# Two uneven stores in place of one: giving four DMA engines more rows at step 56 and at the last step

## The chip, the cores and the metric

The kernel runs on one core of one Trainium2 chip. The time is that of the device in microseconds (us), first as the median of a kernel's runs. "Span" is the time from the first to the last instruction of the profiled execution; it is about 1.8 us shorter than that execution's time.

## The reference

Inputs `q` and `k` are float32 of (16, 512, 16, 64): batch, sequence, heads, dimension. Both are rotated, then each position's heads are multiplied with all positions of the same head:

```python
q_rot = concatenate([q1 * cos - q2 * sin, q1 * sin + q2 * cos], axis=-1)   # k alike
scores = einsum('bshd,bthd->bsht', q_rot, k_rot)                          # (16, 512, 16, 512) float32
```

The output is 268 MB, the inputs 67 MB.

## The kernel before

There are 64 steps (`NST`), 16 batches of 4 (`C`). A step makes 128 rows of 16 heads of 512 scores, 4 MB, in one of three stage buffers in turn, so step i may write its scores only when the store of step i - 3 has landed. For each pair of heads TensorE (PE) multiplies, and ScalarE (ACT) copies the scores from PSUM to the stage.

```python
        for i in range(C, NST):
            ...
            st = stage(i)                       # one of three buffers
            for p in range(HP):
                scores(slot("q", i)[:, P * p : P * (p + 1)], block("k", b, p), st[:, 2 * p : 2 * p + 2])
                ...                             # transposes and rotations for later steps
            store(i, st)
            ...                                 # two of four steps load q or k of a later batch
```

From step 4 on, every store but the last is one transfer of 128 rows (the first four steps, of the first batch, store in two parts). The last leaves two heads of its rows to transfers of their own:

```python
    def last(o, st):
        h = H - 2
        nc.sync.dma_start(o[:, :h], st[:, :h])           # 128 rows of 14 heads: all 16 DMA engines
        nc.sync.dma_start(o[:116, h:], st[:116, h:])     # 116 rows: 29 on each of four engines
        nc.sync.dma_start(o[116:, h:], st[116:, h:])     # 12 rows: one on each of twelve engines
    def store(i, st):
        b, c = divmod(i, C)
        if i == NST - 1:
            last(o_v[b, :, c], st)
        else:
            nc.sync.dma_start(o_v[b, :, c], st)
```

The comments say what the trace of this kernel shows at the last store: 8 long rows on every engine, thirty 4 KB rows (29 and one) on four engines, one on each of eight more, none on the last four.

Of the kernel before, what the change touches and what calls it, by code (L numbers as in the profile page):

```python
# [10 lines left out]
def kernel(  # L11
# [13 lines left out]
    B, S, H, D = q.shape  # L25
# [3 lines left out]
    HP = H // 2  # L29
    NST = B * C  # L30
    G = H // C
    R = H - G

    const_pool = ctx.enter_context(tc.tile_pool(name="const", bufs=1))
# [11 lines left out]
    o_v = out.rearrange("b (p c) h t -> b p c h t", c=C)  # L46
# [4 lines left out]
    ss_t = const_pool.tile([P, C, 2, HD], fp32, name="ss_t")  # L51
    ss_v = ss_t.rearrange("p c x j -> p c (x j)")

    def last(o, st):

        h = H - 2
        nc.sync.dma_start(o[:, :h], st[:, :h])
        nc.sync.dma_start(o[:116, h:], st[:116, h:])
        nc.sync.dma_start(o[116:, h:], st[116:, h:])



    RW = R * S
    W = H * S
# [5 lines left out]
    def stage(i):  # L70
        at = (3 * RW, 0, W)[(i - C) % 3]
        return stage_t[:, at : at + W].rearrange("p (h t) -> p h t", t=S)

    def store(i, st):
        b, c = divmod(i, C)
        if i == NST - 1:
            last(o_v[b, :, c], st)
        else:
            nc.sync.dma_start(o_v[b, :, c], st)

# [22 lines left out]
    def slot(which, n):  # L103
        if which == "r":
            return first["q"][:, n, G * D :]
        t, c = tiles[which, n]
        return t[:, c]

    def unit(which, n):
        return which != "r" and n < C  # L110

    def rope(which, n):
# [4 lines left out]
        if unit(which, n):  # L117
            x = first[which][:, :, G * D * n : G * D * (n + 1)]
            cs = cos_t.unsqueeze(2).to_broadcast((P, C, 2 * G, HD))
            ss = ss_v.unsqueeze(2).to_broadcast((P, C, G, D))  # L120
            sv, k1, k2 = "p c (g j) -> p c g j", {"j": HD}, {"j": D}
# [51 lines left out]
    def scores(lhs, rhs, so):  # L173


        ps = ps_s_pool.tile([P, 2, S], fp32, tag="ps_s", name="ps")
        for r in range(2):
            nc.tensor.matmul(  # L178
                out=ps[:, r, :].rearrange("s (c t) -> s c t", c=C),
                lhsT=lhs[64 * r : 64 * r + 64],  # L180
                rhs=rhs[64 * r : 64 * r + 64],
                start=True,
                stop=True,
            )
        nc.scalar.copy(  # L185
            out=so.rearrange("s r (t c) -> s r t c", c=C),
            in_=ps.rearrange("s r (c t) -> s r t c", c=C),
        )
# [9 lines left out]
    with tc.manual_schedule():  # L198
# [13 lines left out]
        for p in range(HP):  # L212
            c, hp = divmod(p, 2)
            scores(block("q", 0, hp)[:, c], block("k", 0, hp), st_all[:, 2 * p : 2 * p + 2])
            if hp == 1:
                nc.sync.dma_start(o_v[0, :, c, :G], st_all[:, G * c : G * (c + 1)])
            if p == 3:
# [9 lines left out]
        for i in range(C):  # L227
            st = st_rest[i]
# [3 lines left out]
            else:  # L232
                dve = rope("q", C) + rope("k", C + i) + rope("q", C + 1) + rope("k", 2 * C)
                nxt = [("q", C), ("k", C + i)]
            for p in range(R // 2):
                scores(
# [14 lines left out]
        for i in range(C, NST):  # L251
            b, c = divmod(i, C)
            tr = {}
            if i + 1 < NST:
                tr[1], tr[3] = ("q", i + 1, 0), ("q", i + 1, 1)
            if i + C < NST:
                tr[5], tr[6] = ("k", i + C, 0), ("k", i + C, 1)
            dve = []
            if i + 2 < NST:
                dve += rope("q", i + 2)  # L260
            if i + 1 + C < NST:
                dve += rope("k", i + 1 + C)
            st = stage(i)
            for p in range(HP):
                scores(slot("q", i)[:, P * p : P * (p + 1)], block("k", b, p), st[:, 2 * p : 2 * p + 2])
                if p not in tr:
                    continue
                if tr[p][0] == "q":
                    run(dve[:1])
                    dve = dve[1:]  # L270
                    transposed(*tr[p], nc.vector.tensor_copy)
                else:
                    transposed(*tr[p], nc.scalar.copy)
            run(dve)
            store(i, st)
            if c == 1 and b > 1:
                load("q", b + 2)
            elif c == C - 1:
                load("k", b + 3)
# [30 lines left out]
```

## Time and profile before

| | before |
|---|---|
| time, first three runs | 801.64 us (800.84 to 802.97) |
| span of the profiled run | 800.1 us |
| busy: PE, DVE, ACT | 86%, 68%, 71% |
| moved by DMA | 336.19 MB at 420 GB/s |

How to read it: no compute engine is full, while the row of DMA shares in the slices is at nine tenths or more in all slices but the last. A sixteenth of that share is one DMA engine, and with a mean over sixteen engines the tail of a few of them is hard to see in a slice of 20 us. The lines are in the prediction below; the windows cut around the end are what show it. A packet counts whole in the window in which it starts, so in windows of a microsecond or two the share is rough: one engine at work shows as 0.04 to 0.06.

Two moments are used from here on. **R** is when step 54's store has landed on the slowest engine, which lets step 57's score copies begin; it is the end of the wait that starts at 680.72 in the chain (680.72 + 30.02 = 710.74). **X** is when the engines that wait for step 57's store start it, 722.38 here. The slowest engine is called **L**, and the four engines with thirty of the short rows are "the four". The times of single DMA packets come from the trace's packet records, strung into chains as the prediction tells.

### The profile page before, as it was taken

Reading aid. Unit: us, or ns where it says so; the run is one execution under the profiler, and the core shown is the slowest. Engines: PE = TensorE matmul, PEld = TensorE weight load, DVE = VectorE, ACT = ScalarE, POOL = GpSimd, SP = SyncE. Lnnn points to the kernel's source line nnn. Section 1 sums busy time; section 2 is a strip of 40 time slices with the busy share of each in tenths; the row PEclk is TensorE's granted clock in tenths of the full one; section 3 lists DMA queues with packets and bytes.
Section 4 is the critical chain, followed back from the end, with each engine's and each line's share of the span. In section 5 each row is a group of like instructions: output and inputs, shape, how many; then the busy total and the mean of one; then the engine's idle time right before and its main releaser. Section 6 shows DMA issues by size and latency. Waiting matters only on the chain.

```text
span 800.1 us, 8186 instructions
## 1 busy us (share of the span) xinstructions
PE 688.1 (86%) x3072; PEld 298.5 (37%) x3072; DVE 541.6 (68%) x510; ACT 564.1 (71%) x655; POOL 0.7 (0%) x6
## 2 busy tenths in 40 slices
PE   1999999978889978998889888898988979889960
PEld 1444443433334433443333333343433334334420
DVE  4999988856677756785666866667666677577300
ACT  1898887767677756777667676676866768668870
POOL 0000000000000000000000000000000000000000
PEclk9999999989998988998989989899898998899995
DMA  9999999999999999999999999999999999999996
GB/s 369 418 434 429 433 435 426 427 417 430 430 435 430 426 427 427 437 433 424 430 432 428 436 423 439 423 435 427 435 428 434 410 425 436 405 391 396 421 420 249
DMA packets 15158, 336.19 MB, mean 420 GB/s; under 512 B 1680, under 2 KB 1936, under 8 KB 2320
## 3 DMA queue, kind: packets, MB, share of 16 engines
q1 hardware_dynamic: 14832, 335.55, 98.3%
q8 instruction: 24, 0.39, 0.2%
q10 hardware_dynamic: 288, 0.13, 0.1%
q14 instruction: 14, 0.11, 0.0%
HBM read 67.24 MB, written 268.44 MB: 420 GB/s over the span
## 4 chain that ended last, share of the span: by engine, by line
DMA 46%; PE 45%; ACT 5%; issue 1%; DVE 0%; ACTq 0%; SPq 0%; DVEq 0%
DMA out_dram<-st 45%; PE ps L178 34%; PE bank L170 11%; ACT st L185 4%; DMA st<-in_k_dram 1%; ACT st L171 0%; ACTq L305 0%; DVE st L148 0%; DVE st L144 0%; DVE part L143 0%; SPq L99 0%; ACTq L185 0%; DVEq L143 0%
## 5 line engine op out<-in xcount | busy, mean ns | idle before, releaser
L185 ACT COPY st<-ps 128x1024 f32<-128x1024 f32 x512 | 495.1, 1019 | 197.3 <-DMA out_dram<-st 102.8
L178 PE MATMUL ps<-k_sb,q_sb 64*128 64x512 f32 x1920 | 513.7, 652 | 71.3 <-ACT st L185 71.3
L178 PEld LDWEIGHTS ps<-k_sb,q_sb 64*128 64x128 f32 x1920 | 172.4, 197 | 248.2 <-issue 137.9
L171 DVE COPY q_sb<-bank 128x512 f32<-128x512 f32 x118 | 81.5, 691 | 202.3 <-PE bank L170 202.3
L170 PEld LDWEIGHTS bank<-ident,q_sb 128*128 128x128 f32 x480 | 55.6, 152 | 102.3 <-issue 100.0
L170 PE MATMUL bank<-ident,q_sb 128*128 128x128 f32 x480 | 86.7, 308 | 0.0
L170 PEld LDWEIGHTS bank<-ident,k_sb 128*128 128x128 f32 x480 | 50.5, 141 | 91.2 <-DVE k_sb L144 39.6
L170 PE MATMUL bank<-ident,k_sb 128*128 128x128 f32 x480 | 78.0, 286 | 0.0
L144 DVE TENSOR_TENSOR k_sb<-k_sb,cos_t 128x1024 f32<-128x1024 f32 x60 | 73.5, 1225 | 2.9
L144 DVE TENSOR_TENSOR q_sb<-q_sb,cos_t 128x1024 f32<-128x1024 f32 x60 | 73.5, 1225 | 2.1
L148 DVE TENSOR_TENSOR k_sb<-k_sb,part 128x1024 f32<-128x1024 f32 x60 | 73.5, 1225 | 2.1
L143 DVE TENSOR_TENSOR part<-q_sb,ss_t 128x1024 f32<-128x1024 f32 x60 | 73.5, 1225 | 2.0
L143 DVE TENSOR_TENSOR part<-k_sb,ss_t 128x1024 f32<-128x1024 f32 x60 | 72.9, 1216 | 0.2
L148 DVE TENSOR_TENSOR q_sb<-q_sb,part 128x1024 f32<-128x1024 f32 x60 | 72.9, 1215 | 0.1
L171 ACT COPY k_sb<-bank 128x512 f32<-128x512 f32 x120 | 71.4, 600 | 0.0
L178 PE MATMUL ps<-st 64*128 64x512 f32 x128 | 32.7, 639 | 0.4 <-ACT st L171 0.4
L170 PE MATMUL bank<-ident,st 128*128 128x128 f32 x64 | 10.7, 317 | 16.7 <-DVE st L148 13.2
L171 ACT COPY st<-bank 128x512 f32<-128x512 f32 (+1 forms) x18 | 9.2, 566 | 13.7 <-PE bank L170 13.7
L143 DVE TENSOR_TENSOR part<-st,ss_t 128x1024 f32<-128x1024 f32 (+1 forms) x9 | 10.0, 1106 | 10.5 <-DMA st<-in_k_dram 9.2
L178 PEld LDWEIGHTS ps<-st 64*128 64x128 f32 x128 | 11.7, 197 | 13.7 <-issue 8.0
L170 PEld LDWEIGHTS bank<-ident,st 128*128 128x128 f32 x64 | 8.2, 161 | 21.9 <-issue 16.4
L148 DVE TENSOR_TENSOR st<-st,part 128x512 f32<-128x512 f32 (+1 forms) x14 | 10.3, 765 | 0.3
(11 smaller groups left out, 13.8 us busy)
## 6 DMA issues: line engine op xcount, KB each, us to landing
out_dram<-st SPq DMA_DIRECT2D x59, 4096.0 KB, 24.7
k_sb<-in_k_dram SPq DMA_DIRECT2D x15, 2048.0 KB, 28.3
q_sb<-in_q_dram SPq DMA_DIRECT2D x15, 2048.0 KB, 26.9
out_dram<-st SPq DMA_DIRECT2D x4, 3072.0 KB, 18.3
out_dram<-st SPq DMA_DIRECT2D x4, 1024.0 KB, 12.4
out_dram<-st SPq DMA_DIRECT2D x1, 3584.0 KB, 21.4
st<-in_q_dram SPq DMA_DIRECT2D x1, 2048.0 KB, 11.9
st<-in_k_dram SPq DMA_DIRECT2D x2, 512.0 KB, 5.4
```

Of the source, the lines that this page charges most:

```text
L143: nc.vector.tensor_tensor(pv, xs, ss, op=mult)
L144: nc.vector.tensor_tensor(xc, xc, cs, op=mult)
L148: nc.vector.tensor_tensor(y, y, z, op=add)
L170: nc.tensor.transpose(bank[:, y, :], x[:, y], ident)
L171: copy(out=x, in_=bank[:, :m])
L178: nc.tensor.matmul(out=ps[:, r, :].rearrange("s (c t) -> s c t", c=C), lhsT=lhs[64 * r : 64 * r + 64], rhs=rhs[64 * r : 64 * r + 64], star ...
L185: nc.scalar.copy(out=so.rearrange("s r (t c) -> s r t c", c=C), in_=ps.rearrange("s r (c t) -> s r t c", c=C),)
```

## The change

It means to take bytes off L in a second place: at step 56, whose store is followed by a time in which most DMA engines wait (the DMA share is 0.24 from 719.4 to 721.0 us and 0.06 from 721.0 to 722.3), and a little more in the last store. The whole of it:

```diff
+    UNEVEN = {NST - 8: 2, NST - 1: 3}
...
-    def last(o, st):
-
-        h = H - 2
+    def uneven(o, st, heads):
+
+        h = H - heads
         nc.sync.dma_start(o[:, :h], st[:, :h])
         nc.sync.dma_start(o[:116, h:], st[:116, h:])
         nc.sync.dma_start(o[116:, h:], st[116:, h:])
...
-        if i == NST - 1:
-            last(o_v[b, :, c], st)
+        if i in UNEVEN:
+            uneven(o_v[b, :, c], st, UNEVEN[i])
```

## The prediction

> **What bounds the kernel now.** I read the page first: the slices, the chain that ended last, the DMA queues.
>
> ```profile
> PE   1999999978889978998889888898988979889960
> ...
> DMA  9999999999999999999999999999999999999996
> GB/s 369 418 434 429 433 435 426 427 417 430 430 435 430 426 427 427 437 433 424 430 432 428 436 423 439 423 435 427 435 428 434 410 425 436 405 391 396 421 420 249
> ...
> q1 hardware_dynamic: 14832, 335.55, 98.3%
> q8 instruction: 24, 0.39, 0.2%
> ...
> DMA out_dram<-st 45%; PE ps L178 34%; PE bank L170 11%; ACT st L185 4%; DMA st<-in_k_dram 1%; ACT st L171 0%; ACTq L305 0%; DVE st L148 0%; DVE st L144 0%; DVE part L143 0%; SPq L99 0%; ACTq L185 0%; DVEq L143 0%
> ```
>
> The 16 DMA engines are busy in nearly every slice; the load is 336 MB and cannot shrink. What can be lost is only the time in which some of the 16 are idle. So I looked at the end, in windows, reading the DMA share times 16 as the number of engines still at work.
>
> ```profile
> 717.00:718.00 1.00, 1.00 (x8) 0.72 (x8) 0.96 (x2) 1.00 (x2) 0.00 (x0) 1.00 0.54 229
> 718.00:719.40 1.40, 1.40 (x10) 0.54 (x8) 1.37 (x2) 1.31 (x3) 0.00 (x0) 1.00 0.33 140
> ...
> 721.00:722.30 1.30, 1.30 (x8) 0.43 (x5) 0.34 (x1) 1.30 (x2) 0.00 (x0) 1.00 0.06 25
> ...
> 781.00:789.50 8.50, 0.00 (x0) 0.00 (x0) 0.00 (x0) 0.00 (x0) 0.00 (x0) 0.50 1.00 429
> ...
> 792.00:795.20 3.20, 0.00 (x0) 0.00 (x0) 0.00 (x0) 0.00 (x0) 0.00 (x0) 0.50 0.32 113
> ...
> 796.30:798.50 2.20, 0.00 (x0) 0.00 (x0) 0.00 (x0) 0.00 (x0) 0.00 (x0) 0.50 0.04 15
> 798.50:800.10 1.60, 0.00 (x0) 0.00 (x0) 0.00 (x0) 0.00 (x0) 0.00 (x0) 0.50 0.00 0
> ```
>
> From 781 to 789.5 us compute has ended and all sixteen engines stream. From 792 to 795.2 the share is 0.32: five engines. From 796.3 to 798.5 it is 0.04: one engine alone. The last 1.6 us are the landing and the program's end. So one straggler sets the end, and four others follow it closely.
>
> The trace's records of single DMA packets say who they are. A packet of a row starts 3 to 4 ns before the one ahead of it on its engine ends, so they can be strung into chains. The straggler, which I call L, ends the store of step 62 at 789.61 us, where the others end it at 781.4; then it moves eight 28 KB rows, one 4 KB row, and ends at 798.50. L has exactly one 4 KB row; four chains have thirty, and end at 795.28, 795.64, 796.20 and 796.25; the rest end at 790 to 792. L ends the stores of steps 57, 58, 59 and 60 at 740.15, 750.13, 760.13 and 770.06, with no idle time, at 10.0 us a store against 9.7 for the others (its packets of 32 KB took 1213 to 1251 ns, most others' 1213). It is behind because it is a little slower all along, and it has not waited since well before 600 us. Its bytes are the bound.
>
> The other engines wait for L, by way of the stage buffers:
>
> ```profile
> 680.72 30.02 DMA out_dram<-st
> ...
> 750.21 20.38 DMA out_dram<-st
> 770.58 0.02 issue
> 770.61 0.04 ACTq L185
> ```
>
> In the chain of waits the score copy of step 57 starts only when the store of step 54 has landed on L, at 710.7; that of step 63 when step 60's has, at 770.6. The late start of step 57 makes the hole at 717 to 722.4 us: the share falls to 0.06, only L at work, and fifteen engines start step 57's store within 143 ns at 722.4.
>
> [...] 4 KB rows took 159 ns when undisturbed and up to 727 at 790 us, and L's last eight 28 KB rows took 1062, 1069, 1062, 1062, 1180, 1076, 1062 and 1178 ns, 255 ns more than eight of 1062.
>
> **The change, part by part.** Nothing moves on PE, DVE or ACT; the queue of SP gets two more transfers at step 56. In KB for each engine:
>
> - Step 56 was 8 rows of 32 KB, 256 for all. Now 8 x 28 = 224, plus 29 x 4 = 116 and 4 on engines 0 to 3 (344), plus 4 on engines 4 to 11 (228); engines 12 to 15 have 224.
> - Step 63 already was 344, 228 and 224. Now 8 x 26 = 208, plus 29 x 6 + 6 = 180 on engines 0 to 3 (388), plus 6 (214), or 208.
> - Together +132 KB for engines 0 to 3, -28 - 14 = -42 for 4 to 11, where L is, and -48 for 12 to 15. The total is unchanged (4 x 132 = 8 x 42 + 4 x 48).
>
> L's gain: at step 56 eight rows go from 1213 to 1062 ns, 1.21 us less, and a 4 KB row of 0.16 is added: 1.05. At step 63 eight rows lose another 2 KB each; 4 KB are 151 ns (1213 less 1062), so 75 ns a row, 0.60 us, less 0.07 for the longer single row: 0.53. Sum 1.58. [...] L should end 1.2 us earlier, near 797.3. All of it is on the path, as L never waits.
>
> Engines 0 to 3 at step 63: eight rows of 26 KB at 987 ns are 7.9 us instead of 8.5, so they reach their extra rows at 789.35 instead of 789.95. The thirty rows took 5.3 to 6.3 us before, where thirty undisturbed ones at 155.5 ns would take 4.7: 1.14 to 1.35 times. Rows of 6 KB should start 231 ns apart (159 + 75.5 - 3.5), thirty of them 6.9 us, and 7.9 to 9.3 with that hindrance. They end at 797.2 to 798.7, if step 56 leaves them nothing to catch up.
>
> Step 56 gives them 88 KB more, 30 x 0.156 - 8 x 0.151 = 3.5 us. Nine engines ended step 56 at 717.9 us and then idled 4.5 until 722.4: for such an engine it is all hidden. The later stores leave almost no idle time (0.1 to 0.4 us before steps 58 and 59, none after), so nothing else can absorb it.
>
> So on my main path the end goes from 798.5 to the later of L, 797.3, and the slowest of the four, near 798: half a microsecond less. 801.6 becomes about 801.1.
>
> **Rivals.**
>
> 1. The four take over as the bound by more. Four engines of the sixteen ended step 56 not at 717.9 but at 721.1 to 721.3. If these are engines 0 to 3, only 1.1 us of idle time is left, of 3.5, and the rest collides with step 57's packets; some 2.4 to 3 us, less 0.6 of later holes, is carried to the end, which becomes about 800.4: 1.9 us slower, 803.5. For it: a group of just four that keep together. Against it: the trace does not number the engines, the hole cuts the chains at 722.4, and other groups of four fit as well. I give it a quarter.
> 2. [...] L gains nothing. For it: the 1180 and 1178 ns packets. Against it: 255 ns for eight rows, not 1200. It would make 801.6 to 802.
> 3. Everything goes well: the four's rows are hindered as little as the best chain was, and L's gain is whole. End 796.9 to 797.3, 800.2.
> 4. The extra issues delay the queue. Step 63's took 0.33, 0.71 and 1.21 us on SP, and SP waits for ACT 654 us in all; step 57 is issued 10 us later. Nothing.
>
> **Range and chances.** Weighing 1 at a quarter, 2 at a fifth and the main path and 3 for the rest gives 801.1 in the middle, with more room above. The three runs of before spread by 2.1 us, as much as the effect itself. The range that should hold 8 times in 10 is 799.6 to 802.9. A change of 2% would be 16 us, ten times the 1.58 us that L sheds, so within 2% is 0.99, and 0.005 for each side.
>
> **What would show it.** In the windows after the last issue, the time with one engine alone (0.04 to 0.06) should go or be short, and five engines (about 0.3) should be at work until some 797. At 717 to 722 us the share should rise to five engines or so instead of falling. L's last packet should end near 797.3 and the landing of step 60 come about 0.8 us earlier than 770.6. If the four end after 799 rival 1 holds; if L's end does not move, rival 2. The prediction is wrong altogether if L is another engine in the next execution, one of the first four, say, or if its lag comes from something that the bytes do not govern.

No trace numbers the engines. "Engines 0 to 3", "4 to 11" and "12 to 15" are names of the groups that the trace shows: four engines with thirty 4 KB rows, eight with one (L among them), four with none. That step 56's store would divide in the same way was a forecast; the changed kernel's trace shows four chains that move thirty 4 KB rows there and end at 721.5 to 721.7. L's gain came to 1.58 us, less 0.4, the estimate of further delay: the 255 ns by which L's last eight rows exceeded eight of 1062 ns, once more at step 56, and half as much at step 63. That leaves 1.2, and L's end near 797.3.

## The result, and the profile after

| | before | after |
|---|---|---|
| median of six runs each | 801.51 us (800.84 to 802.97) | 801.83 us (799.68 to 804.69) |
| ratio | | 1.0003, 95% interval 0.998 to 1.0026 |
| span of the profiled run | 800.1 us | 800.5 us |
| L's last byte, us of the span | 798.50 | 797.02 |
| last byte of the four | 796.25 | 798.65 |

The ratio is the mean time of one kernel's fast runs over that of the other's of the same rounds, so it is not quite the ratio of the two medians.

The changed kernel's windows, of the same kind as the prediction shows for the kernel before (stretch, its length, busy time of PE, PEld, DVE, ACT and POOL, granted clock, DMA share, GB/s):

```profile
717.30:719.40 2.10, 2.10 (x12) 0.88 (x10) 2.06 (x2) 1.69 (x2) 0.00 (x0) 0.83 0.56 232
...
720.50:721.70 1.20, 1.20 (x8) 0.61 (x8) 1.17 (x2) 1.20 (x2) 0.00 (x0) 1.00 0.28 113
721.70:723.80 2.10, 2.10 (x12) 0.82 (x9) 0.56 (x1) 1.96 (x3) 0.00 (x0) 1.00 0.06 27
...
792.00:796.80 4.80, 0.00 (x0) 0.00 (x0) 0.00 (x0) 0.00 (x0) 0.00 (x0) 0.50 0.31 123
797.05:798.20 1.15, 0.00 (x0) 0.00 (x0) 0.00 (x0) 0.00 (x0) 0.00 (x0) 0.50 0.25 102
798.70:800.50 1.80, 0.00 (x0) 0.00 (x0) 0.00 (x0) 0.00 (x0) 0.00 (x0) 0.50 0.01 5
```

Before, one engine was alone at the end (0.04 from 796.3 to 798.5). Now, after L is done at 797.02, the share is 0.25: four engines of sixteen. In the hole after step 56 the share is 0.28 up to 721.7, five engines: L and the four with their extra rows. Then L is alone, 0.06, until X at 723.91. So the four's extra work of step 56 was hidden in full, and their extra work of step 63 made them the last.

The chain of waits shows R, 681.81 + 29.26 = 711.07:

```profile
681.81 29.26 DMA out_dram<-st
711.17 1.02 ACT st L186
```

From R on, the two traces can be compared step by step on L, which has no idle time in either:

| L, us | before | after |
|---|---|---|
| step 56's store | 9.98 (720.15 to 730.13) | 8.92 (720.46 to 729.38) |
| steps 57 to 62 | 59.48 | 59.53 |
| step 63 | 8.89 | 8.11 |
| end, counted from R | 87.76 | 85.95 |

L sheds 1.06 + 0.78 us, and ends 1.8 us earlier counted from R. The four end 0.18 us before L's old place: 798.65 - 711.07 = 87.58. That is nearly all of the gain given back.

### The profile page after: what moved, and what is told of

Same layout as the page of the kernel before. It is cut to its first block, busy times and chain, and to the rows that moved or that the text cites. A ratio compares the mean times of both kernels' runs of the same rounds, so it can differ in the third digit from the quotient of the medians.

```text
span 800.5 us, 8190 instructions
## 1 busy us (share of the span) xinstructions
PE 690.9 (86%) x3072; PEld 300.2 (38%) x3072; DVE 541.6 (68%) x510; ACT 564.4 (71%) x655; POOL 0.7 (0%) x6
## 4 chain that ended last, share of the span: by engine, by line
PE 46%; DMA 45%; ACT 4%; DVE 2%; issue 1%; ACTq 0%; SPq 0%; DVEq 0%
DMA out_dram<-st 43%; PE ps L179 35%; PE bank L171 11%; ACT st L186 3%; DMA st<-in_q_dram 1%; DVE st L149 1%; DVE part L144 1%; DVE st L145 1%; ACTq L306 0%; SPq L100 0%; ACTq L186 0%; ACT st L172 0%; DVEq L144 0%
## 5 line engine op out<-in xcount | busy, mean ns | idle before, releaser
L145 DVE TENSOR_TENSOR k_sb<-k_sb,cos_t 128x1024 f32<-128x1024 f32 x60 | 73.5, 1225 | 2.9
L145 DVE TENSOR_TENSOR q_sb<-q_sb,cos_t 128x1024 f32<-128x1024 f32 x60 | 73.5, 1225 | 2.1
L149 DVE TENSOR_TENSOR k_sb<-k_sb,part 128x1024 f32<-128x1024 f32 x60 | 73.5, 1225 | 2.1
L144 DVE TENSOR_TENSOR part<-q_sb,ss_t 128x1024 f32<-128x1024 f32 x60 | 73.5, 1225 | 2.0
L144 DVE TENSOR_TENSOR part<-k_sb,ss_t 128x1024 f32<-128x1024 f32 x60 | 73.0, 1216 | 0.2
L179 PEld LDWEIGHTS ps<-st 64*128 64x128 f32 x128 | 11.4, 192 | 13.4 <-issue 7.6
```

The costliest lines, as they stand in the source:

```text
L144: nc.vector.tensor_tensor(pv, xs, ss, op=mult)
L145: nc.vector.tensor_tensor(xc, xc, cs, op=mult)
L149: nc.vector.tensor_tensor(y, y, z, op=add)
L179: nc.tensor.matmul(out=ps[:, r, :].rearrange("s (c t) -> s c t", c=C), lhsT=lhs[64 * r : 64 * r + 64], rhs=rhs[64 * r : 64 * r + 64], star ...
```

## The experiments

Twelve runs were made. Nine change only the table of uneven stores or cut the 12-row transfers, and three repeat a kernel unaltered. Counted from R or X, with the granted clock of TensorE as the mean of the 8 us after R:

| trace | heads at step 56 / 63 | R | clock after R | X - R | L - R | four - X | end - R |
|---|---|---|---|---|---|---|---|
| before | 0 / 2 | 710.74 | 0.79 | 11.6 | 87.76 | 73.9 | 87.76 |
| before, again | 0 / 2 | 712.38 | 1.00 | 10.1 | 87.75 | 73.8 | 87.75 |
| changed | 2 / 3 | 711.07 | 0.57 | 12.8 | 85.95 | 74.7 | 87.58 |
| changed, 2nd | 2 / 3 | 712.21 | 1.00 | 10.1 | 87.21 | 77.1 | 87.21 |
| changed, 3rd | 2 / 3 | 712.72 | 0.79 | 11.5 | 85.95 | 75.8 | 87.27 |
| none | 0 / 0 | 714.67 | 0.79 | 11.7 | 88.55 | - | 88.55 |
| step 56 alone | 2 / 2 | 715.41 | 0.79 | 11.7 | 87.29 | 73.7 | 87.29 |
| longer last alone | 0 / 3 | 709.42 | 0.57 | 13.1 | 86.99 | 75.6 | 88.67 |
| step 57 for 56 | 2 at 57 / 3 | 713.54 | 0.57 | 11.4 | 85.96 | 79.5 | 90.97 |
| three and two | 3 / 2 | 710.62 | 0.57 | 12.8 | 86.69 | 73.5 | 86.69 |
| three and two, 2nd | 3 / 2 | 710.79 | 0.79 | 11.7 | 86.97 | 74.4 | 86.97 |
| four and one | 4 / 1 | 711.44 | 0.79 | 11.7 | 86.89 | 79.1 | 90.81 |

R differs by 6 us between executions, although the kernels differ in nothing before step 56's store, which is issued 3 to 9 us before R and which L moves after those of steps 54 and 55 (in the first trace of before these end on L at 710.74 and 720.15, step 56's at 730.13). The two traces of before alone differ by 1.6 us. In the columns above, "four" is the slowest of the four. The scatter of R goes into the time whole; the columns that start from R or X do not have it. (With step 57 uneven, X is a little early for its clock, since the first 14 heads are issued ahead of the rest, at 724.13 against 725.78.)

### No uneven store

```diff
-    UNEVEN = {NST - 8: 2, NST - 1: 3}
+    UNEVEN = {}
```

> No store is uneven; every engine gets 256 KB of each store. Theory (the end is the later of the straggler L and of engines 0 to 3): L gets back the 28 KB that step 63 took from it, [...] so it ends 0.8 to 1.05 us later than in the kernel before, and the four end with the others near 790; time 802.4, one engine alone from 790 on. Rival (the engines' shares do not matter[...]): within 0.3 us of the kernel before.

(28 KB are 1.05 us; less up to 0.25, the 255 ns measured in the kernel before, that is 0.8.)

805.34 us, ratio 1.0043 (1.0014 to 1.0073). L ends at R + 88.55, 0.79 later than before: at the lower edge of what was expected. In its trace L alone is at work for the last 4.4 us, a share of 0.05:

```profile
798.80:803.20 4.40, 0.00 (x0) 0.00 (x0) 0.00 (x0) 0.00 (x0) 0.00 (x0) 0.50 0.05 22
```

L's eight packets of the last store took 1213 ns each, none longer. The median is 3 us above what was expected. In the profiled execution (806.29 us) R came 3.9 us later than in the first trace of before, which accounts for that one; the other five have no trace, so for them the excess is left open. The uneven last store is worth 0.8 us on L in the trace.

### Step 56 alone

```diff
+    UNEVEN = {NST - 8: 2, NST - 1: 2}
```

> Step 56 as in the changed kernel, step 63 as in the kernel before. Theory: L sheds 28 KB more than before, so it ends 0.8 to 1.05 us earlier; the extra 3.5 us of engines 0 to 3 fall into the hole before step 57 and are hidden, so these end 2 us ahead of L as before; 800.6. Rival (step 56's extra is not hidden): the four end 2 to 3.5 us later than before and set the end, 802 or more.

801.76 us, ratio 1.0009 (0.9982 to 1.0037), not the 800.6 expected. In the profiled execution (806.39 us) R was 4.7 us later than in the first trace of before. Step 56 took L 8.98 us, 1.0 less than before, and the four, though they ended step 56 0.8 us past X, end as in the kernel before (X + 73.7): hidden. But one of L's packets in the last store took 1762 ns where 1062 is undisturbed, and two more 24 and 130 ns more, so that its end is only 0.47 us earlier from R. The rival fell; the gain was half lost to something that the first trace of before showed smaller (255 ns).

### The longer last store alone

```diff
+    UNEVEN = {NST - 1: 3}
```

> Step 56 even, step 63 with three heads. Theory: L ends 0.5 us earlier than before, the four 1.7 to 2.2 us later, so they come out about equal, near 798.0 of a trace; 801.0 to 801.5. Rival (the last store's longer rows are what undid the gain of the changed kernel): as slow as the changed kernel, 801.8.

801.13 us, ratio 1.0006 (0.9979 to 1.0033): not to be told from either. The trace is clearer: L ends at R + 86.99, 0.77 earlier than before, and the four at R + 88.67, 1.7 later than L. So the third head in the last store makes the four the last engines by itself, and undoes what it brings. The rival's mechanism held, though not its time.

### The same bytes, after the hole in place of before it

```diff
+    UNEVEN = {NST - 7: 2, NST - 1: 3}
```

> The changed kernel with step 57 uneven in place of step 56, just after the hole. Same bytes on each engine as in the changed kernel. Theory: the four have no idle time left to hide 3.5 us in (0.1 to 0.4 us at two steps), so they end about 3 us later than in the changed kernel, 804.8, with four engines at work after L has ended for some 4 us. Rival (only the sum of bytes per engine counts): as the changed kernel, 801.8.

806.11 us, ratio 1.0064 (1.0035 to 1.0093). Every engine moves as much as in the changed kernel, but the four end at X + 79.5 in place of 74.7, that is 3.4 us later from R. Once L is done at 799.50, four engines work on, then two:

```profile
799.55:802.30 2.75, 0.00 (x0) 0.00 (x0) 0.00 (x0) 0.00 (x0) 0.00 (x0) 0.50 0.26 107
802.70:803.80 1.10, 0.00 (x0) 0.00 (x0) 0.00 (x0) 0.00 (x0) 0.00 (x0) 0.50 0.12 50
```

The sum of bytes per engine does not decide; where the extra bytes fall does.

### Three heads at step 56, two at the last

```diff
+    UNEVEN = {NST - 8: 3, NST - 1: 2}
```

> Step 56 with three heads and step 63 with two: on every engine the same sum of bytes as in the changed kernel, but the larger share falls into the hole before step 57. Theory: L as in the changed kernel (1.0 to 1.6 us earlier than before), the four end step 56 some 1.7 us later than in the changed kernel, near 723.4 of its trace, still inside or at the edge of the hole, and do about 0.9 us less at the end; so they no longer set the end; about 1 us faster than the changed kernel, 800.5 to 801. In the trace the four should end before L or within 0.5 us of it. Rival (only the sum of bytes counts): as the changed kernel.

801.21 us, ratio 0.9999 (0.9966 to 1.0033). The time says nothing, the trace holds what was expected of it: the four are done with step 56 at X, 723.4 (the share is 0.30, five engines, to 722.6), five engines work on together near the end, and then no store is left (the 0.02 is of another queue):

```profile
720.30:722.60 2.30, 2.30 (x13) 1.06 (x12) 1.48 (x2) 2.15 (x4) 0.00 (x0) 1.00 0.30 127
...
792.50:796.00 3.50, 0.00 (x0) 0.00 (x0) 0.00 (x0) 0.00 (x0) 0.00 (x0) 0.50 0.32 114
797.35:799.20 1.85, 0.00 (x0) 0.00 (x0) 0.00 (x0) 0.00 (x0) 0.00 (x0) 0.50 0.02 4
```

L is last again, at R + 86.69; two of its packets took 1661 and 1189 ns in place of 1062.

### The changed kernel a second time

> The changed kernel unaltered, for its scatter and a second trace. Theory: the four end after L by some 0.5 us or more where the score copies of step 57 come late after the hole (halved clock), and about with L where they come early; the median within 1.5 us of the kernel before either way. L should again have no idle time and take about 9 us for step 56 in place of 10.

801.37 us, ratio 0.9999 (0.9971 to 1.0027). Here the clock was full after R, X came only 10.1 us after it, and the four were still at step 56's rows until 725.5, past X at 722.3: they did not fit in the hole. Three of them end by 798.54. The fourth, one of whose 26 KB rows took 1889 ns in place of 987, ends at 799.40 = X + 77.1, and L with it, at 799.42, since its last three long rows took 1345, 1448 and 1194 ns in place of 987, 1.0 us in all. So here delays on L and the late one of the four both ate the gain, 0.55 us being left.

TensorE's mean clock in the 8 us after R, first in the kernel before, then in the changed kernel's first and second trace (the column before the DMA share):

```profile
710.74:718.74 8.00, 6.84 (x25) 2.82 (x25) 4.19 (x4) 6.13 (x7) 0.00 (x0) 0.79 0.86 369
```

```profile
711.07:719.07 8.00, 6.83 (x20) 2.82 (x20) 3.61 (x4) 5.21 (x6) 0.00 (x0) 0.57 0.85 366
```

```profile
712.21:720.21 8.00, 6.84 (x34) 3.12 (x36) 5.44 (x6) 7.64 (x9) 0.00 (x0) 1.00 0.92 380
```

TensorE is busy for the same 6.84 us each time, and issues 25, 20 and 34 matmuls in it. The records of the granted clock show it halved for 3.41 us in the first, 6.83 us in the second, and not at all in the third. The gap between matmuls that R ends was 2.68, 3.94 and 1.51 us; in the changed kernel's third trace it was 4.90 us, with a clock of 0.79. What halves the clock is not shown. X - R is 11.6, 12.8 and 10.1 us. The hole in which the four hide their rows is that long or short.

### Numbering L, first try

```diff
-        nc.sync.dma_start(o[116:, h:], st[116:, h:])
+        t2 = S // 2
+        if heads == 3:
+            marks = [(6, h, 0, S), (8, h + 1, 0, S), (7, h + 2, 0, S)]
+        else:
+            marks = [(9, h, 0, S), (10, h + 1, 0, t2), (11, h + 1, t2, S)]
+        for k, g, x, y in marks:
+            nc.sync.dma_start(o[116:116 + k, g, x:y], st[116:116 + k, g, x:y])
+            nc.sync.dma_start(o[116 + k:, g, x:y], st[116 + k:, g, x:y])
```

> The changed kernel with the 12-row transfers cut into pieces of 6+6, 8+4 and 7+5 rows (step 63) and 9+3, 10+2 and 11+1 rows (step 56), so that the number of small packets and of completion packets that the straggler L carries tells its number among engines 4 to 11. [...] Time as the changed kernel or up to 1 us more.

810.54 us in one run, 8 us worse than expected: a failed experiment, by its own doing. The queue of SP, with the six pieces of step 56's 12 rows (lines 66 and 67) and then step 57's store (line 87):

```profile
711.26 0.86 SPq L67 DMA_DIRECT2D out_dram<-st  x1
712.76 0.29 SPq L66 DMA_DIRECT2D out_dram<-st  x1
722.79 0.23 SPq L67 DMA_DIRECT2D out_dram<-st  x1
731.60 40.55 SPq L87 DMA_DIRECT2D out_dram<-st  x6
```

and SP's waits of the same run (who waited for whom: us in total, times, longest), where for step 57's store of the other kernels SP waited for ACT alone:

```profile
SPq L67 <- DMA out_dram<-st: 14.8, 2, 9.7
...
SPq L87 <- DMA out_dram<-st: 8.5, 1, 8.5
```

The sixth piece waited 9.7 us for an earlier store to land, and step 57's store 8.5 us more. This wait is the program's own. The trace's instruction records name the semaphore that each transfer counts up: SP's are eight, used in turn, and in this run the two transfers that follow were issued only when the earlier one of their semaphore had landed. The sixth piece shares its semaphore with step 55's store, which landed at 722.78 (the piece was issued at 722.79), and step 57's store with the first transfer of step 56, which landed at 731.53 (issued at 731.60). X was 732.45 in place of about 724. At step 56 L carried three small packets after its long rows; which engine that makes it is not shown. At step 63 L could not be told apart: all sixteen engines began step 57's store within 150 ns, and from then on no engine took 10.0 us a store: single ones fell behind once, by 1 to 2 us, and then kept the pace of 9.7. So whichever engine had been L now kept the others' pace.

### Three and two, a second time

> Three heads at step 56, two at step 63, a second time. Let R be the moment when step 54's store has landed on L and lets step 57's score copies go, and X the moment when the fifteen other engines start step 57's store. Theory: L ends at R + 86 to 86.9 [...], the four at X + 73.5 to 73.9 as in the other kernels with two heads at the end; X - R is 10.3, 11.7 or 13 us as TensorE's clock after its idle time is full, 0.8 or 0.57. The end of the DMA is R + 86.0 to 87 against R + 87.8 in the kernel before. The whole time scatters with R, which the change does not touch. Rival (the two kernels' ends do not differ once R is taken out): R + 87.6 or more.

801.19 us, ratio 1.0005 (0.9971 to 1.0039). The end is at R + 86.97, L's, with 1.02 us of delays in its last store (one packet of 1947 ns); the four end at X + 74.4, a little past the 73.9 expected, having been late for X by 2 us at step 56.

### The changed kernel a third time

> The changed kernel a third time. Theory: L at R + 86.0 to 87.2; the four at X + 74.7 to 75.6, so that they are the later ones where X - R is 13 and about even where it is less; the end at R + 87.2 to 88.6. Rival: the four never matter, the end is L's in all traces.

801.07 us, ratio 0.999 (0.9964 to 1.0016). L at R + 85.95, the four at R + 87.27 and X + 75.8. As in the first trace, the four are last, here by 1.3 us.

### Four heads at step 56, one at the last

```diff
+    UNEVEN = {NST - 8: 4, NST - 1: 1}
```

> Four heads at step 56, one at step 63, the same sum of bytes per engine again. Theory: the four end step 56 about 1.7 us later than with three heads, so 0.5 to 3 us after X, and carry that on, but their last store is 0.9 to 1.7 us shorter; the two cancel or nearly so, and they end about as with three and two. [...] end R + 85.8 to 86.8. Rival (the hole does not limit what can be hidden): 0.9 us or more faster than three and two.

803.56 us, ratio 1.0026 (0.9996 to 1.0056). Worse than all of that: the four ended step 56 at 728.5 to 729.7, 5 to 7 us after X (0.5 to 3 had been expected), stayed that late, and one of them had a packet of 30 KB that took 3838 ns where 1138 is usual. The end is at R + 90.81, while the other three were done at R + 88.1 and L at R + 86.89. What did not fit in the hole (X - R was 11.7 us) was carried to the end. Both the theory's number and the rival's were wrong here.

### Numbering L, second try

```diff
     UNEVEN = {NST - 8: 3, NST - 1: 2}
...
-        nc.sync.dma_start(o[116:, h:], st[116:, h:])
+        k = 116 + (7 if heads == 2 else 8)
+        nc.sync.dma_start(o[116:k, h:], st[116:k, h:])
+        nc.sync.dma_start(o[k:, h:], st[k:, h:])
```

> Three and two heads, with the 12-row transfers cut in 7+5 at step 63 and 8+4 at step 56, to number L with fewer small transfers. [...] With 18 transfers after step 54 where the first trial had 24, none should have to wait for an earlier one, so step 57's store is issued as early as in the changed kernel.

800.89 us in one run. Nothing waited on SP. L carried one small packet at step 56 (8 + 4 rows) and two at step 63 (7 + 5 rows). No run shows which number that gives it, so L stays without one. It ended at R + 87.5, with 1.4 us of such delays.

### The kernel before, a second time

> The kernel before, unaltered, for a second trace of it. With R the landing of step 54's store on L and X the start of step 57's store on the others: theory: L without idle time at R + 87.5 to 88.5 [...], about 10 us for step 56; the four at X + 73.5 to 74.3, ahead of L; the end is L's. Rival (the difference of 0.2 to 0.6 us between the ends of the two kernels, taken from R, is only the scatter of one trace): the end at R + 87.2 or less.

Its ratio to the kernel before, of which it is a copy, came out as 0.9965 (0.9933 to 0.9997), with a median of 800.1 against 802.52 us. A comparison of six runs with eleven thus "found" 3 us between two equal kernels. In the trace everything held: L at R + 87.75 (87.76 in the first trace), the four at X + 73.8, the last 3.6 us L's alone:

```profile
796.30:799.90 3.60, 0.00 (x0) 0.00 (x0) 0.00 (x0) 0.00 (x0) 0.00 (x0) 0.50 0.06 24
```

## Why the prediction was right or wrong

The time was right: 801.1 forecast, 801.83 measured, in the range. Over all, 56 runs of the kernel before have a mean of 801.83 and 18 of the changed kernel 801.73 us, with standard deviations of 2.0 and 1.5; the difference, 0.1, has a standard error of 0.44 (the root of 2.0 squared over 56 plus 1.5 squared over 18). The half microsecond forecast is neither confirmed nor refuted by times. Nor does the hit say much: the range would have held the unchanged kernel's 801.51 as well. By its steps:

- **L is the bound of the kernel before: right.** Two traces give R + 87.76 and 87.75, with L alone at the end.
- **L's gain, 1.58 less 0.4: right in size (1.2 forecast; 1.81, 0.55 and 1.81 measured), but the 0.4 for delays was no constant.** In the two traces with 1.81 L lost nothing where it had lost 255 ns before; in the other it lost 1.0 us. (L ended step 60 at 769.35 in the first trace, 0.7 us earlier than before, as forecast.) In the kernels with a 2-head last store the loss was 0.23 to 1.42 us, in those with 3 heads under 0.02 us in four traces of five, and zero in the one trace with even stores. What delays L is not shown. Longer extra rows mostly went with less loss, and in three traces (both of the kernel before, and step 56 alone) L's last long row took 1178 to 1192 ns in place of 1062 when no other store packet was under way. Nor did any run isolate the cause.
- **The four reach 797.2 to 798.7: 798.65, but by luck, as two misses cancelled.** The slowest one's thirty rows took 7.5 us, less than the 7.9 to 9.3 forecast. But X was 1.5 us later than in the kernel before, which the forecast did not know; without that they would have ended near 797.1.
- **Step 56's extra is hidden: right in two traces of three.** It was done 2.2 us before X in the first trace and 0.1 us after X in the third. In the second, where TensorE's clock stayed full and X came early, it ran 3.2 us over, which is the course of rival 1. The prediction had put the length of the hole at a fixed 4.5 us and did not see that it differs with the clock after TensorE's wait (X - R was 12.8, 11.5 and 10.1 us at clocks of 0.57, 0.79 and 1.00, in the first, third and second trace). That is the term it missed.
- **On the main path the end goes from 798.5 to the later of L and the four, half a microsecond less: right in kind, and in size in two traces of three.** Counted from R the end came 0.18, 0.55 and 0.49 us earlier. Where the rest of L's 1.8 us went is shown: to the four in the first and third trace (they end 1.6 and 1.3 us after L), to delays on L and on one of the four alike in the second.
- **Rival 2, that L gains nothing: fell** in the two traces in which L gained 1.81 us.
- **Rival 4, that more issues cost nothing: right for three transfers, wrong as a rule.** In the first numbering try, with six pieces in place of step 56's third transfer, SP stopped for 9.7 us, for a semaphore still in use.
- **"It is behind because it is a little slower all along": not so.** In the first numbering try, where all sixteen started step 57 together, no engine was slow after that. Nor is L slow throughout elsewhere. In the trace with even stores its chain can be followed back to 677.8 us: its 32 KB rows took 1213 ns up to 712.9 and 1216 to 1274 from then to the last score copy. In the eleven traces followed, they took 1245 to 1251 ns on average while scores were still computed and copied, and 1214 to 1217 after the last copy (777 to 782 us). (The prediction read up to 1251 ns; the longest row from step 56 on in its own trace took 1284.) What slows L in that stretch, and why this engine is the one, stays open.

The experiment with step 57 is the strongest evidence for the mechanism, as the same bytes per engine cost 1.0064 against 1.0003. A version with three heads at step 56 and two at the end has the earliest end from R, 86.69 and 86.97 (87.5 with its 12 rows cut for the numbering) against 87.21 to 87.58 for the changed kernel and 87.76 for the kernel before: 0.3 to 1.1 us better than the kernel before, a tenth of a per cent. In times, at 801.21 and 801.19 us, it cannot be told from either, and it is not claimed to be faster.

## What to carry to other kernels

When a transfer-bound kernel waits for one late DMA engine, taking bytes off it pays only until the engines that get them are the next to be late (in the first trace L ended 1.81 us earlier from R, and the four kept all but 0.18 of it): compute the end of both groups, and put the extra bytes where the receivers would be idle. Measure a change of a tenth of a per cent from a common event inside the trace, not from the whole time, when that event scatters by more than the change; and run the unchanged kernel against itself to know how far the ratio wanders.
